# Row statistics between value remainders, and a deferred log of the forget gates, in a hybrid attention layer

## The chip, the cores and the metric

The kernel runs on one core of a Trainium2 chip. The metric is the device time of one execution in microseconds (us); lower is better. The engines are PE (TensorE, matrix products; PEld is its loading of weights), DVE (VectorE), ACT (ScalarE), POOL (GpSimd) and SP (SyncE, which here issues DMAs). Each takes its own instructions in order, and semaphores join them. "The profile" is one execution recorded by the chip's profiler; lines such as L516 are lines of the kernel before.

## What is computed

One layer of a streaming encoder on a sequence of 1024 rows of width 1024, in float32: a modulated layer norm, one input projection, two groups of eight attention heads of width 64 (forgetting attention and stick-breaking attention), a gate on each head, an output projection, and a layer norm over the residual. Cut to what matters:

```python
mod = silu(c) @ w_ada + b_ada                      # shift, scale, gate
u = layer_norm(x) * (1 + scale) + shift
fq, fk, fv, fg, ff, sq, sk, sv, sg = split(u @ w_in)
log_f = log_sigmoid(ff + b_f)                      # 8 forget gates for each row
f_cum = cumsum(log_f, axis=1)
# forgetting attention, causal:   softmax(q k / 8 + f_cum[q] - f_cum[k]) v
# stick-breaking, strictly causal: z = q k / 8
#   w = exp(log_sigmoid(z) + sum of log_sigmoid(-z) over later keys);  w v
y = concat(fox * silu(fg), sb * silu(sg)) @ w_out
x = layer_norm(2 ** 0.25 * x + gate * y, ln_g, ln_b)
```

## The kernel before

**Precision.** Every float32 product is made of three or four passes over split operands: a rounded high part and a remainder. The rounding is a copy on ACT (sometimes POOL), the remainder a subtraction on DVE or POOL. A result in a bank of PSUM is therefore read first by ACT (rounded part) and then by DVE (accumulator minus rounded part). Two readers of one bank take turns.

**Order.** The order on PE is as the program is written, from start to end (`manual_schedule`); that on SP too, up to L856. On ACT, DVE and POOL a planner that simulates the time line at build picks the order among the instructions that it takes to be ready. `after(a, b)` adds an edge without a semaphore: what is issued inside stands, on the engine of `a`, behind `a`. It fixes an order and nothing more.

**The start.** Eight row tiles of 128 rows of x. For each, `norm_stats(t)` takes two `bn_stats` halves of 512 columns and one aggregate on DVE (L197, L198, L189), then the inverse square root on POOL (L191, L192), and `norm_x(t)` normalises in place, on DVE for tiles 6 and 7 (L217), else on ACT (L218). Tiles 0 to 3 make the first half of u, over which five projection accumulators are built (loop at L683, `start_steps`). In that loop's step `kb == 5` stand the statistics of tiles 4 and 5, in step 6 those of tiles 6 and 7, behind the step's last remainder `rest`. Then PE makes the values of row tiles 0 to 3 (`v_first`, L798 to L810). One such block is 24 matmuls (L355 to L357). Its evacuation is four instructions in turn: rounding on ACT (L363), remainder on DVE (L364), for each of two head pairs; they are put into `v_evacs`. Blocks 0 and 2 lie in the two halves of the tile `st_late`, block 1 in one of two "T" banks. Between the blocks stand `norm_x(5..7)`, behind `v_evacs` of block 0, and `late_round(0)` and `late_round(1)`: four transposes of tiles 4 to 7 (L242) each, into T banks, rounded on ACT and DVE. The second of these takes the T bank of value block 1.

**The main loop** runs over 128 units (pair, head, row tile i). For a unit k of the first four pairs (stick-breaking) PE first transposes the weights of unit k-2 (L514, at most four blocks to a T bank, two T banks), with a weights-times-values product (L531) in between, and then makes the scores S of unit k (L462, L463). Two sigmoids on ACT (L484, L486) empty S, a scan on DVE (L491, L495) and a product on POOL (L497) make the weights. The transposes are rounded on ACT (L516), and their remainder is taken on DVE (L517), which frees the T bank. S has one buffer: the next unit's scores wait for both sigmoids. Behind each unit come filler steps: the remaining projections, cut into steps of three matmuls by generators (`gen_m`: two empty steps, then 16; `gen_v`). `FILL` sets the steps of each pair (52, 72, 68, 68, ...), spread over its 16 units about evenly (`W0` = 100), `LEAD` = 2 half units ahead.

**The forget gates.** `gen_forget` runs beside the projections of pairs 2 and 3, one of its steps after each of theirs. Its input `fsb` is complete with the last value block of group 1 (filler step 122). It takes max(-f, f) on DVE (L388), then a sigmoid and its logarithm on ACT (L389, L390; the logarithm isn't in the table of functions that the sigmoid uses, so ACT loads another, and loads the first back at the next sigmoid), waits `FLOG` = 8 steps, adds min(f, 0) (L394) and scans over row tiles (L397), waits `FROW` = 16 steps, builds a triangle of ones on POOL in a slot of the ring that the attention tiles use (L401 to L405), sums over rows on PE (L407, L408), transposes (L414), and stores the sums to DRAM from SP (L416). They are read back when pair 4 begins.

Of the kernel before, what the change touches and what calls it, by code (L numbers as in the profile page):

```python
# [10 lines left out]
AF = mybir.ActivationFunctionType  # L11
# [16 lines left out]
def tile_hybrid_layer(  # L28
# [17 lines left out]
    nc = tc.nc  # L46
# [9 lines left out]
    def att_tile(name, dt=F32):  # L56
        return big("att", 6, name, dt)
# [10 lines left out]
    def t_tile(name):  # L68
        return ps.tile([P, 512], F32, tag="T", bufs=2, name=name)

    def s_tile(name):
        return ps.tile([P, 2, 512], F32, tag="S", bufs=1, name=name)

    RING = 5
    WARM = (4, 1, 1, 1, 1)
    NORM_ON = {6: nc.vector, 7: nc.vector}
    FLOG = 8
    FROW = 16
    GATE = 20
# [3 lines left out]
    def after(*instructions):  # L83
        stack = ExitStack()
        for i in instructions:
            stack.enter_context(tc.issue_after(i.ins))
        return stack
# [54 lines left out]
    c_sb = cp.tile([P, NB], F32, tag="c_sb", name="c_sb")  # L142
    xt, wss_sb, late_x = [], [], []
# [22 lines left out]
    cm = cp.tile([P, NB], F32, tag="cm", name="cm")  # L166
# [15 lines left out]
        nc.tensor.matmul(sc_all[:, kt // 4, kt % 4 * P:][:, :P], sc[:, kt:kt + 1].to_broadcast([P, P]), ident,  # L182
                         start=True, stop=True)

    powed = [None]

    def ln_finish(st, name):
        mv = sb.tile([P, 2], F32, tag="mv", bufs=3, name=f"mv_{name}")
        nc.vector.bn_aggr(mv, st)  # L189
        rs = sb.tile([P, 2], F32, tag="rs", bufs=3, name=f"rs_{name}")  # L190
        nc.gpsimd.tensor_scalar_add(rs[:, 0:1], mv[:, 1:2], EPS)  # L191
        powed[0] = nc.gpsimd.tensor_tensor(rs[:, 0:1], rs[:, 0:1], mhalf, op=ALU.pow)  # L192
        return mv, rs

    def ln_stats(src, name):
        st = sb.tile([P, 3, 6], F32, tag="st", bufs=3, name=f"st_{name}")[:, :2, :]
        nc.vector.bn_stats(st[:, 0, :], src[:, 0:512])  # L197
        nc.vector.bn_stats(st[:, 1, :], src[:, 512:1024])  # L198
        return ln_finish(st, name)


# [3 lines left out]

    norm = {}

    def norm_stats(t):
        mv, rs = norm[t] = ln_stats(xt[t], f"a{t}")
        if t not in NORM_ON:  # L210
            nc.gpsimd.tensor_scalar(rs[:, 1:2], mv[:, 0:1], rs[:, 0:1], -1.0, op0=ALU.mult, op1=ALU.mult)

    def norm_x(t, a=0, b=D):
        mv, rs = norm[t]
        xs = xt[t][:, a:b]
        if t in NORM_ON:
            return NORM_ON[t].tensor_scalar(xs, xs, mv[:, 0:1], rs[:, 0:1], op0=ALU.subtract, op1=ALU.mult)  # L217
        return nc.scalar.activation(xs, xs, AF.Identity, scale=rs[:, 0:1], bias=rs[:, 1:2])  # L218
# [4 lines left out]
    def in_turn(make, *args):  # L223
        with after(*turn_of):
            turn_of[:] = [make(*args)]
        return turn_of[0]
# [116 lines left out]
    v_evacs = []  # L343
# [40 lines left out]
    def gen_forget():  # L384
        ff = fsb.rearrange("p h t -> p (h t)")
        ab = cp.tile([P, 64], F32, tag="fab", name="fab")
        lf = flf[:, 1:]
        nc.vector.scalar_tensor_tensor(ab, ff, -1.0, ff, op0=ALU.mult, op1=ALU.max)  # L388
        nc.scalar.activation(ab, ab, AF.Sigmoid)  # L389
        nc.scalar.activation(ab, ab, AF.Ln)  # L390
        for _ in range(FLOG):
            yield
        with after(*lows):
            nc.vector.scalar_tensor_tensor(lf, ff, 0.0, ab, op0=ALU.min, op1=ALU.add)  # L394

        pre = ff
        nc.vector.tensor_tensor_scan(pre, flf[:, 0:64], later.rearrange("p h t -> p (h t)"), initial=0.0,  # L397
                                     op0=ALU.add, op1=ALU.mult)
        for _ in range(FROW):
            yield  # L400
        scratch = att_tile("fscratch")  # L401
        tri, fr = scratch[:, :P], scratch[:64, P:2 * P]
        nc.gpsimd.memset(tri, 1.0)
        nc.gpsimd.affine_select(out=tri, in_=tri, pattern=[[1, P]], base=0,
                                channel_multiplier=-1, compare_op=ALU.is_ge, fill=0.0)  # L405
        fp = t_tile("fcum")[:, :64]
        nc.tensor.matmul(fp, tri, lf, start=True, stop=False)  # L407
        nc.tensor.matmul(fp, ones.to_broadcast([P, P]), pre, start=False, stop=True)  # L408
        fc = cp.tile([P, 64], F32, tag="fab", name="fc")
        nc.scalar.activation(fc, fp, AF.Copy, scale=-1.0)  # L410
        yield
        yield
        ft = t_tile("frow")[:64, :P]
        nc.tensor.transpose(ft, fc, ident)  # L414
        nc.scalar.copy(fr, ft)
        nc.sync.dma_start(f_dr.rearrange("h (t p) -> (h t) p", p=P), fr)  # L416
        yield
# [17 lines left out]
        r = slice(h * HD, h * HD + HD)  # L435
        nc.scalar.copy(z[r, :], qst[p][h].bitcast(F32)[r, i * P:i * P + P])  # L436

    masks, scaled, lows = [], [], []

    def att_causal(u):  # L440
        p, h, i = u
        if p >= 4:
            if not masks:
                masks.append(pv_tile("causal_ps", 1)[:, :P])
                nc.vector.tensor_copy(masks[0], causal)
            f = fb[2 * (p - 4) + h]
            dg = slice(i * P, i * P + P)
            nc.vector.tensor_tensor(f[:, dg], f[:, dg], masks[0], op=ALU.add)

    def att_scores(u, following):  # L450
        p, h, i = u
        z = zq.pop(u)
        ke = (i + 1) * P
        ns = 1 if ke <= 512 else 2
        w = ke // ns
        qs = slice(i * P, i * P + P)
        if p >= 4:
            f = fb[2 * (p - 4) + h]
        S = s_tile(f"S_{p}_{h}_{i}")
        for s in range(ns):  # L460
            ks = slice(s * w, s * w + w)
            nc.tensor.matmul(S[:, s, :w], qst[p][h][:, qs], kst[p][h][:, ks], start=True, stop=False)  # L462
            nc.tensor.matmul(S[:, s, :w], z, klo[p][:, ks], start=False, stop=True)  # L463
        v3 = lambda a: a[:, :ke].rearrange("p (a b) -> p a b", a=ns)
        if p >= 4:
            a = att_tile(f"a_{p}_{h}_{i}")
            nm = sb.tile([P, 1], F32, tag="nm", bufs=4, name=f"nm_{p}_{h}_{i}")
            l = sb.tile([P, 1], F32, tag="l", bufs=4, name=f"l_{p}_{h}_{i}")
            with after(*lows):
                nc.vector.tensor_tensor_reduce(out=v3(a), in0=S[:, :ns, :w], in1=v3(f),  # L470
                                               op0=ALU.add, op1=ALU.min, scale=-1.0, scalar=BIG,
                                               accum_out=nm)
            if following:
                att_causal(following)
            nc.scalar.activation(a[:, :ke], a[:, :ke], AF.Exp, scale=-1.0, bias=nm, accum_out=l)  # L475
            nc.vector.reciprocal(l, l)  # L476
            scaled[:] = [*scaled[-3:],
                         nc.gpsimd.tensor_scalar(a[:, :ke], a[:, :ke], l, 1.0, op0=ALU.mult, op1=ALU.mult)]  # L478
            st_w[u] = a
        else:  # L480
            kp = att_tile(f"kp_{p}_{h}_{i}")
            be = att_tile(f"be_{p}_{h}_{i}")
            with after(*key_casts):
                nc.scalar.activation(v3(kp), S[:, :ns, :w], AF.Sigmoid, scale=-1.0)  # L484
            key_casts.clear()
            last_act = nc.scalar.activation(v3(be), S[:, :ns, :w], AF.Sigmoid)  # L486


            lo = max(ke - 512, 0)
            rv = kp[:, lo:ke][:, ::-1]  # L490
            last_dve = nc.vector.tensor_tensor_scan(rv, rv, floor[:, :ke - lo], initial=0.0,  # L491
                                                    op0=ALU.mult, op1=ALU.max)
            if lo:
                rv = kp[:, :lo][:, ::-1]
                last_dve = nc.vector.tensor_tensor_scan(rv, rv, floor[:, P:P + 1].to_broadcast([P, lo]),  # L495
                                                        initial=kp[:, lo:lo + 1], op0=ALU.mult, op1=ALU.max)
            nc.gpsimd.tensor_tensor(be[:, :ke - 1], be[:, :ke - 1], kp[:, 1:ke], op=ALU.mult)  # L497
            nc.gpsimd.memset(be[:, ke - 1:ke], 0.0)
            st_w[u] = be
            return last_act, last_dve  # L500
# [182 lines left out]
    for kb in range(NB):  # L683
# [18 lines left out]
        else:  # L702
# [3 lines left out]
            rest = in_turn(u_rest, kb + 1)  # L706
# [33 lines left out]
            norm_stats(5)  # L740
            norm_x(4)
        if kb == 6:
            with after(rest):
                for t in (6, 7):
                    norm_stats(t)
            make_v(0)

    wg = {}
# [45 lines left out]
    def v_first(t, acc):  # L794
        for _ in v_tile(0, t, acc, v0_w):
            pass

    v_first(0, late_acc[:, 0, :])  # L798
    with after(*v_evacs):
        for t in (5, 6, 7):  # L800
            norm_x(t)
# [12 lines left out]
    for kb in range(NB):  # L814
# [9 lines left out]
        if kb < len(evacs):  # L824
            n, h = evacs[kb]
# [5 lines left out]
    first = nc.scalar.copy(held[:, :512], acc1[0])  # L831
# [343 lines left out]
```

## Time and profile before

| | us |
|---|---|
| median of 3 runs | 682.38 (682.34 to 682.41) |
| the profiled execution | 682.39 |
| its span, first to last instruction | 680.6 |
| granted clock of PE, mean | 0.997 |
| all waits of PE in its list, sum of five | 3.0 |

A timeline row reads: start, length, engine, line, operation, tile written <- tiles read, shapes, how many instructions are merged, and in brackets the idle time before it with what ended it. The ends of matmuls are modelled (a 128x512 one is listed with 0.39 and the next starts 0.23 later), so distances between starts say more than lengths. A row of the waits reads: who waited for whom, total us, times, the longest. Where a wait is on several semaphores, the one that came last is named, and it need not be the one that mattered.

### The profile page before, as it was taken

What the parts mean: (1) busy time and instruction counts of PE and PEld (TensorE: products, weight loads), DVE (VectorE), ACT (ScalarE), POOL (GpSimd) and SP (SyncE); (2) the same over time, 40 slices, a digit from 0 to 9 for tenths busy, and PEclk for the clock granted to TensorE, in tenths of its full rate; (3) what the DMA queues carried; (4) which work ended last, traced back from release to release, by engine and by line L of the source; (5) the groups of instructions that cost most, each with busy time, mean ns of one, the idle gap of its engine ahead of it and who ended that gap; (6) DMA issues with size and microseconds to landing.
All of it is one profiled execution on the core that took longest, in us unless ns stands there. A gap on an engine that the chain in (4) does not pass through costs nothing.

```text
span 680.6 us, 11191 instructions
## 1 busy us (share of the span) xinstructions
PE 670.2 (98%) x3713; PEld 571.7 (84%) x3713; DVE 484.8 (71%) x996; ACT 380.1 (56%) x857; POOL 406.1 (60%) x530
## 2 busy tenths in 40 slices
PE   8999999999999999999999999999999999999995
PEld 5788898888997888889988888889988888888885
DVE  6787779868666777777676675766676777885645
ACT  6567368756566666666665564656565766521000
POOL 5550279756357656566369778786795365655412
PEclk9999999999999999999999999999999999999998
DMA  9983432112102122122134454363352297153301
GB/s 332 401 309 117 140 76 77 41 29 59 34 11 66 41 54 56 40 54 55 32 109 144 147 165 156 106 192 118 118 178 59 60 361 299 59 178 105 119 32 62
DMA packets 46472, 81.54 MB, mean 120 GB/s; under 512 B 5264, under 2 KB 20176, under 8 KB 46416
## 3 DMA queue, kind: packets, MB, share of 16 engines
q1 hardware_dynamic: 44832, 76.37, 34.6%
q10 hardware_dynamic: 1584, 4.47, 2.1%
q8 instruction: 29, 0.48, 0.3%
q14 instruction: 27, 0.22, 0.1%
HBM read 60.34 MB, written 16.29 MB: 113 GB/s over the span
## 4 chain that ended last, share of the span: by engine, by line
PE 94%; DVE 2%; ACT 1%; POOL 1%; issue 0%; POOLq 0%; DVEq 0%
PE m L297 10%; PE m L298 10%; PE m L299 10%; PE pv L531 10%; PE T L514 9%; PE S L463 5%; PE S L462 5%; PE o L917 4%; PE o L915 4%; PE o L916 4%; PE v L355 4%; PE v L357 4%; PE v L356 4%; PE st_late L623 1%; PE st_q L623 1%; PE sc_all L176 1%
## 5 line engine op out<-in xcount | busy, mean ns | idle before, releaser
L517 DVE TENSOR_TENSOR pt<-T,pt 128x512 fp32r<-128x512 f32 (+2 forms) x192 | 102.6, 553 | 43.2 <-ACT pt L516 41.7
L516 ACT CAST pt<-T 128x512 fp32r<-128x512 f32 (+2 forms) x192 | 88.7, 478 | 64.3 <-PE T L514 62.5
L297 PE MATMUL m<-uh,whi 128*128 128x512 f32 x304 | 123.4, 406 | 0.0
L299 PE MATMUL m<-uh,wlo 128*128 128x512 f32 x304 | 119.8, 394 | 0.0
L298 PE MATMUL m<-ul,whi 128*128 128x512 f32 x304 | 119.6, 394 | 0.0
L497 POOL TENSOR_TENSOR be<-be,kp 128x127 f32<-128x127 f32 (+3 forms) x64 | 79.0, 1235 | 37.4 <-DVE kp L495 25.8
L491 DVE TENSOR_TENSOR_SCAN kp<-kp,floor 128x512 f32<-128x512 f32 (+2 forms) x64 | 65.0, 1016 | 25.5 <-ACT kp L484 24.4
L531 PE MATMUL pv<-pt,v 128*128 128x512 f32 x320 | 82.8, 388 | 0.0
L478 POOL TENSOR_SCALAR a<-a,l 128x1024 f32<-128x1024 f32 (+3 forms) x64 | 48.4, 757 | 36.5 <-DVE l L476 27.8
L462 PE MATMUL S<-k,q 128*128 128x512 f32 (+5 forms) x192 | 68.8, 360 | 0.3 <-ACT be L486 0.3
L299 PEld LDWEIGHTS m<-uh,wlo 128*128 128x128 f32 x304 | 57.1, 188 | 13.7
L475 ACT ACTIVATE a<-a,nm 128x1024 f32<-128x1024 f32 (+3 forms) x64 | 49.8, 778 | 29.2 <-DVE nm L470 28.8
L297 PEld LDWEIGHTS m<-uh,whi 128*128 128x128 f32 x304 | 57.2, 188 | 10.1 <-PE T L514 0.3
L463 PE MATMUL S<-kl,qz 128*128 128x512 f32 (+5 forms) x192 | 65.3, 341 | 0.0
L298 PEld LDWEIGHTS m<-ul,whi 128*128 128x128 f32 x304 | 57.3, 188 | 9.0
L531 PEld LDWEIGHTS pv<-pt,v 128*128 128x128 f32 x320 | 55.4, 189 | 9.1
L547 POOL TENSOR_TENSOR ty<-ty,sg 64x256 f32<-64x256 f32 x64 | 47.0, 734 | 24.0 <-issue 11.0
L470 DVE CUSTOM_DVE_ANT_0 a<-S,fb 128x1024 f32<-128x1024 f32 (+3 forms) x64 | 48.2, 753 | 16.8 <-PE S L463 13.1
L436 ACT CAST qz<-q 64x128 fp32r<-64x128 f32 x128 | 37.3, 296 | 33.9 <-PE S L463 32.7
L355 PE MATMUL v<-whi_v,uh 128*128 128x256 f32 (+1 forms) x192 | 54.7, 285 | 0.0
L357 PE MATMUL v<-wlo_v,uh 128*128 128x256 f32 (+1 forms) x192 | 54.2, 282 | 0.0
L484 ACT ACTIVATE kp<-S 128x128 f32<-128x128 f32 (+3 forms) x64 | 42.0, 656 | 21.5 <-PE S L463 20.2
(289 smaller groups left out, 1622.6 us busy)
## 6 DMA issues: line engine op xcount, KB each, us to landing
raw<-in_w_qkg_dram SPq DMA_DIRECT2D x38, 256.0 KB, 2.8
wss<-in_w_ss_dram SPq DMA_DIRECT2D x16, 512.0 KB, 8.5
x<-in_x_dram SPq DMA_DIRECT2D x8, 512.0 KB, 6.6
k<-k SPq DMA_DIRECT2D x32, 128.0 KB, 2.3
wg<-in_w_gate_dram SPq DMA_DIRECT2D x8, 512.0 KB, 4.6
raw_o<-in_w_out_dram SPq DMA_DIRECT2D x16, 256.0 KB, 2.9
fb<-f_dr ACTq DMA_DIRECT2D x8, 512.0 KB, 4.4
wo_dr<-whi_o SPq DMA_DIRECT2D x16, 256.0 KB, 2.1
```

The source lines that it names most:

```text
L297: nc.tensor.matmul(acc, hi[:, c], u_hi[kt][:, s], start=(kt == 0), stop=False)
L298: nc.tensor.matmul(acc, hi[:, c], u_lo[kt][:, s], start=False, stop=False)
L299: nc.tensor.matmul(acc, lo[:, c], u_hi[kt][:, s], start=False, stop=(kt == NB - 1))
L355: nc.tensor.matmul(acc[:, :n], u_hi[kt][:, ts_], hi[:, s], start=(kt == 0), stop=False)
L357: nc.tensor.matmul(acc[:, :n], u_hi[kt][:, ts_], lo[:, s], start=False, stop=(kt == NB - 1))
L462: nc.tensor.matmul(S[:, s, :w], qst[p][h][:, qs], kst[p][h][:, ks], start=True, stop=False)
L463: nc.tensor.matmul(S[:, s, :w], z, klo[p][:, ks], start=False, stop=True)
L491: last_dve = nc.vector.tensor_tensor_scan(rv, rv, floor[:, :ke - lo], initial=0.0, op0=ALU.mult, op1=ALU.max)
L497: nc.gpsimd.tensor_tensor(be[:, :ke - 1], be[:, :ke - 1], kp[:, 1:ke], op=ALU.mult)
L516: nc.scalar.copy(hi[:, :n, qo:qo + P], t3)
L517: lows[:] = [nc.vector.tensor_tensor(lo[:, :n, qo:qo + P], t3, hi.bitcast(F32)[:, :n, qo:qo + P], op=ALU.subtract)]
L531: nc.tensor.matmul(acc2[:, :, q0:], vt[p][:, kb, h * P:(h + 1) * P], pt[:, :, q0:], start=(kb == 0), stop=(kb == last))
```

## The change

Two edits. First, the statistics at the start. The two halves of `ln_stats` can each be put behind instructions of their own. Tile 6's statistics stand behind tile 5's aggregate as well; tile 7's leave the loop and come after the first value block: the first half behind that block's first remainder (`v_evacs[1]`) and tile 6's aggregate, the second half behind its second remainder (`v_evacs[3]`).

```diff
-    powed = [None]
+    powed, aggr = [None], [None]
     def ln_finish(st, name):
...
-        nc.vector.bn_aggr(mv, st)
+        aggr[0] = nc.vector.bn_aggr(mv, st)
...
-    def ln_stats(src, name):
+    def ln_stats(src, name, behind):
         st = sb.tile([P, 3, 6], F32, tag="st", bufs=3, name=f"st_{name}")[:, :2, :]
-        nc.vector.bn_stats(st[:, 0, :], src[:, 0:512])
-        nc.vector.bn_stats(st[:, 1, :], src[:, 512:1024])
+        for h, first in enumerate(behind):
+            with after(*first):
+                nc.vector.bn_stats(st[:, h, :], src[:, h * 512:h * 512 + 512])
         return ln_finish(st, name)
...
-    def norm_stats(t):
-        mv, rs = norm[t] = ln_stats(xt[t], f"a{t}")
+    def norm_stats(t, *behind):
+        mv, rs = norm[t] = ln_stats(xt[t], f"a{t}", behind or ((), ()))
...
         if kb == 6:
-            with after(rest):
-                for t in (6, 7):
-                    norm_stats(t)
+            with after(rest, aggr[0]):
+                norm_stats(6)
             make_v(0)
...
     v_first(0, late_acc[:, 0, :])
+    norm_stats(7, (v_evacs[1], aggr[0]), (v_evacs[3],))
     with after(*v_evacs):
```

Second, the forget gates. The sigmoid and the logarithm come seven filler steps later, behind the latest unit's second sigmoid (`gates`, set in `att_scores`), and a small sigmoid of 8 columns, whose result nobody reads, is issued behind the logarithm. All that follows in `gen_forget` moves by the same seven steps.

```diff
+    FGATE = 7
...
         nc.vector.scalar_tensor_tensor(ab, ff, -1.0, ff, op0=ALU.mult, op1=ALU.max)
-        nc.scalar.activation(ab, ab, AF.Sigmoid)
-        nc.scalar.activation(ab, ab, AF.Ln)
+        for _ in range(FGATE):
+            yield
+        with after(*gates):
+            nc.scalar.activation(ab, ab, AF.Sigmoid)
+            logs = nc.scalar.activation(ab, ab, AF.Ln)
+        with after(logs):
+            nc.scalar.activation(cm, c_sb, AF.Sigmoid)
         for _ in range(FLOG):
             yield
...
-    masks, scaled, lows = [], [], []
+    masks, scaled, lows, gates = [], [], [], []
...
             last_act = nc.scalar.activation(v3(be), S[:, :ns, :w], AF.Sigmoid)
+            gates[:] = [last_act]
```

## The prediction

> **What bounds the kernel now.** I read the page's busy times first, then the waits of PE over the whole span.
>
> ```profile
> PE 670.2 (98%) x3713; PEld 571.7 (84%) x3713; DVE 484.8 (71%) x996; ACT 380.1 (56%) x857; POOL 406.1 (60%) x530
> PE sc_all L176 <- POOL ident masks.py:199: 1.6, 1, 1.6
> PE st_late L355 <- DVE v L364: 0.5, 1, 0.5
> PE st_q L623 <- ACT uh L255: 0.3, 1, 0.3
> PE T L514 <- POOL wlo L127: 0.3, 1, 0.3
> PE S L462 <- ACT be L486: 0.3, 1, 0.3
> ```
>
> PE is busy 98% of the span, and all that it waits for is five places. Its instructions run in the order in which they are written, so a wait that goes shortens the span by its length, unless PE then meets another. Two places belong to the change: the value block at 51 us (L355) and the pair L514, L462 near 213 us. A listed wait counts from a modelled end. What PE really loses I take from starts in the timeline of PE. First the value blocks of 24 matmuls each:
>
> ```profile
> 44.79 0.28 PE L355 MATMUL st_late<-v_home,uh 128*128 128x256 f32 x1
> ...
> 47.63 0.28 PE L355 MATMUL v<-v_home,uh 128*128 128x256 f32 x1
> ...
> 50.37 0.28 PE L357 MATMUL v<-v_w,uh 128*128 128x256 f32 x1
> 51.15 0.39 PE L355 MATMUL st_late<-v_home,uh 128*128 128x256 f32 x1 [0.50 <-DVE v L364]
> ...
> 54.09 1.03 PE L242 MATMUL xT<-ident,x 128*128 128x128 f32 x8
> ```
>
> The block of row tile 0 takes 47.63 - 44.79 = 2.84, which is 0.12 a matmul. Tile 2's block should start at 50.37 + 0.12 = 50.49 and end at 53.33. It ends at 54.09, so **0.76 us** are lost here. Then the second place, beside the same step one pair later:
>
> ```profile
> 212.20 0.40 PE L299 MATMUL m<-uh,wlo 128*128 128x512 f32 x1
> 212.89 1.06 PE L514 MATMUL T<-ident,be 128*128 128x128 f32 x8 [0.30 <-POOL wlo L127]
> ...
> 214.56 0.40 PE L297 MATMUL m<-uh,whi 128*128 128x512 f32 x1
> ...
> 247.11 0.40 PE L299 MATMUL m<-uh,wlo 128*128 128x512 f32 x1
> ...
> 248.46 0.40 PE L297 MATMUL m<-uh,whi 128*128 128x512 f32 x1
> ...
> 251.24 0.27 PE L514 MATMUL T<-ident,be 128*128 128x128 f32 x1
> ```
>
> From the last projection matmul over eight transposes and two score matmuls to the next projection it is 214.56 - 212.20 = 2.36 here and 248.46 - 247.11 = 1.35 there: **1.01 us** lost. Both places together are 1.77 of 682.39, 0.26%. That is the ceiling of the change; 0.2% (1.36 us) is about what a measurement of this kernel can tell from no change.
>
> **Part 1, the statistics.** Next the timelines of DVE, ACT and POOL at the first place.
>
> ```profile
> 47.60 0.69 DVE L197 BATCH_NORM_STATS2 st_a<-x 128x6 f32<-128x512 f32 x1
> ...
> 48.81 0.19 DVE L189 BATCH_NORM_AGGREGATE mv_a<-st_a 128x2 f32<-128x12 f32 x1
> ...
> 49.47 0.68 DVE L198 BATCH_NORM_STATS2 st_a<-x 128x6 f32<-128x512 f32 x1
> 50.18 0.29 DVE L364 TENSOR_TENSOR v<-st_late,v 128x128 fp32r<-128x128 f32 x1
> ...
> 50.80 0.29 DVE L364 TENSOR_TENSOR v<-st_late,v 128x128 fp32r<-128x128 f32 x1
> 51.62 1.70 DVE L217 TENSOR_SCALAR x<-x,mv_a,rs_a 128x1024 f32<-128x1024 f32 x2 [0.53 <-POOL rs_a L192]
> ...
> 53.85 0.29 DVE L364 TENSOR_TENSOR v<-v,v 128x128 fp32r<-128x128 f32 x1 [0.33 <-ACT v L363]
> ```
>
> ```profile
> 50.50 0.27 ACT L363 CAST v<-st_late 128x128 fp32r<-128x128 f32 x1 [2.00 <-DVE v L364]
> ```
>
> ```profile
> 51.02 1.45 POOL L192 TENSOR_TENSOR rs_a<-rs_a,mhalf 128x1 f32<-128x1 f32 x2
> ```
>
> Four statistics halves (tiles 6 and 7) stand ahead of the first value remainder at 50.18. The second value rounding on ACT waits 2.00 for that remainder, since both read one bank, and the second remainder at 50.80 lets PE go at 51.15, 0.35 after its start. The change removes no instruction and adds none. Tile 5's aggregate goes ahead of tile 6's halves, and tile 7's halves go one behind each remainder. New order on DVE from 47.60: aggregate 5 (0.1 to 0.2), two halves of tile 6 (48.81 - 47.60 = 1.21), so the first remainder starts at about 49.0. ACT's second rounding (0.27) lies beside aggregate 6 (0.2) and the first half of tile 7 (0.68). The second remainder starts near 50.1, and PE may go at 50.1 + 0.35 = 50.45, before its 50.49. The wait goes.
>
> What is late next: PE reaches the eight transposes (L242) 0.76 earlier, at 53.33. The first four read tiles 4 to 7 normalised; the next four write the bank that the remainders of tile 1's values empty, about 0.4 later (half of the eight), at 53.73. From 50.1 DVE still has a remainder (0.29), a half (0.68), aggregate 7 (0.2), two normalisations (1.70) and two remainders (0.58): 3.45, so 53.55 without a gap. Tile 7's scale passes POOL behind aggregate 7 (about 51.2): half of 1.45 for the power, with the addition ahead of it ready near 52.2, so tile 7's normalisation can't end before 53.05. With PE's 0.35 behind the start of the last remainder (53.26) it goes on at 53.6 without gaps on DVE, and at 54.1 if DVE idles 0.5, as it does at 51.62. I take a new wait of 0.2 there: **gain 0.55**, bounds 0 (DVE's chain ends when it did) and 0.76. No DMA is moved in this part.
>
> **Part 2, the logarithm.** ACT and DVE at the second place, and ACT and DVE one pair later:
>
> ```profile
> 209.72 0.26 ACT L389 ACTIVATE fab<-fab 128x64 f32<-128x64 f32 x1 [2.97 <-DVE fab L388]
> 209.99 1.28 ACT L390 ACT_TABLE_LOAD   x1
> ...
> 211.45 0.95 ACT L516 CAST pt<-T 128x512 fp32r<-128x512 f32 x2
> 212.42 1.28 ACT L484 ACT_TABLE_LOAD   x1
> 213.72 0.28 ACT L484 ACTIVATE kp<-S 128x128 f32<-128x128 f32 x1
> ...
> 214.78 0.59 ACT L289 ACTIVATE sg<-m 128x512 f32<-128x512 f32 x1
> ...
> 245.77 0.30 ACT L436 CAST qz<-q 64x128 fp32r<-64x128 f32 x1
> 247.98 1.08 ACT L516 CAST pt<-T 128x512 fp32r<-128x512 f32 x2 [1.91 <-PE T L514]
> ```
>
> ```profile
> 212.05 1.16 DVE L517 TENSOR_TENSOR pt<-T,pt 128x512 fp32r<-128x512 f32 x2 [2.37 <-ACT pt L516]
> ...
> 248.60 1.29 DVE L517 TENSOR_TENSOR pt<-T,pt 128x512 fp32r<-128x512 f32 x2 [1.33 <-ACT pt L516]
> ```
>
> ACT takes instructions in order. The small sigmoid L389 waits 2.97 on DVE, then comes the load for the logarithm, and only at 211.45 the roundings of transposed weights that stand behind them. Their remainders run from 212.05, the first over at about 212.7, and only then has PE a free transpose bank: 212.89. (The wait list names a POOL split; no transpose reads one, and the bank explains the time as well.) The load back, 1.28 at 212.42, holds the sigmoids that empty S, so L462 waits too.
>
> New: the log of the gates began in filler step 123; seven later is step 130, and by FILL and W0 that is the first step behind unit (2,0,0)'s scores (124 steps through pair 1, some 4 for each unit, LEAD half units ahead), so it stands behind that unit's second sigmoid. The block is sigmoid, load, logarithm, load, small sigmoid: 0.26 + 1.28 + 0.26 + 1.28 + at most 0.26 = 3.3 in a row. The added sigmoid costs between 0 and 0.26; I take 0.2. What covers it is the gap that ACT has one pair later at the same spot: from 245.77 + 0.30 to 247.98, 1.91. The rest, 3.3 - 1.9 = 1.4, pushes the roundings behind it. One pair later their first remainder ends at about 248.60 + 0.65 = 249.25, and PE wants the bank at 251.24: 2.0 of slack against 1.4. So 0.6 is left, and none if the tanh of the gate projection (L289, 0.59) also goes ahead. **Gain 0.95**, bounds 0 (the pair of loads is merely moved) and 1.01. The row-sum step (matmuls L407, transpose L414, store to f_dr on SP) moves seven steps too; its matmuls cost PE the same there, and its store is wanted when pair 4 begins.
>
> The page ScalarE: Activation LUTs of the Trainium skill, section What ACT_TABLE_LOAD costs, speaks against this part: it puts a switch at 1.28 of load and 1.38 of drain, 2.66 in all. By that the block would be an estimated 6.1, and the sum would lose some 2 us to a new wait of PE. In the rows the load starts at 209.99, when L389 ends (209.98), and L484 starts at 213.72, when its load ends (213.70), so I use 1.28.
>
> **Sum.** 682.39 - 0.55 - 0.95 = 680.9 (span 679.1). The profiled execution's 682.39 is 0.01 off the median 682.38, so the sum needs no shift.
>
> **Rivals.**
> 1. The start's gain is caught at the transposes: DVE's remainder at 53.85 stays where it is. For it: DVE has only 0.2 to spare of the new times. Against: it idled 0.53 and 0.33 in this stretch. Part 2 alone: 681.4. Chance 0.17.
> 2. The logarithm isn't hidden, the two loads come apart again (the planner may set the small sigmoid behind the next roundings), and PE waits as before: 682.39 - 0.55 = 681.8. Chance 0.14. With it goes a longer switch: if ACT empties ahead of each load and a load costs its 1.28 twice, the roundings come 2 x 1.28 = 2.6 later still, 2.0 beyond the 0.6 that is left: 682.39 - 0.55 - 1.01 + 2.0 = 682.8. Chance 0.03, as the rows show no gap. That is what the page's drain would do.
> 3. Slower: the triangle for the row sums (L403, L404 on POOL) moves to unit (2,0,5) and gets behind that unit's product.
>
> ```profile
> 226.33 0.29 POOL L404 TENSOR_SCALAR_AFFINE_SELECT fscratch<-fscratch 128x128 f32<-128x128 f32 x1
> ...
> 234.05 1.55 POOL L497 TENSOR_TENSOR be<-be,kp 128x767 f32<-128x767 f32 x1 [1.33 <-DVE kp L495]
> ...
> 236.27 1.31 POOL L127 TENSOR_TENSOR wlo<-raw,whi 128x512 fp32r<-128x512 f32 x1
> ```
>
> ```profile
> 233.40 0.39 PE L299 MATMUL m<-uh,wlo 128*128 128x512 f32 x1
> ```
>
> PE wants it at 233.40 + 0.23 = 233.6 on the old clock. Behind the product it is ready no earlier than 235.60 + 0.29 = 235.9, behind the split 237.58 + 0.29 = 237.9: 2.3 to 4.3 lost on top of the forecast, 683.2 to 685.2. It decides once the triangle ends after 233.6. Against: POOL idles 1.33 ahead of the product, and what is ready goes first. Chance 0.08, 0.06 of it above 683.75.
> 4. The planner's new orders on ACT, DVE and POOL open small waits elsewhere that eat the gain, or the instructions don't land where the edges point: 682.3. Chance 0.10, 0.01 beyond +0.2%.
>
> **How the numbers follow.** The forecast, both parts with at least 1.36 of 1.77 kept, has 0.48. Faster by over 0.2% is that alone, 0.48; slower 0.06 + 0.01 = 0.07; the rest, rivals 1, 2 and most of 4, 0.45. The low end is the ceiling, 682.39 - 1.77 = 680.6, less 0.1. The high end takes in rivals 1 and 2 and half of 4: 682.4. Outside lie the 0.08 of rival 3, the 0.03, half of rival 4 and a little below.
>
> **What would show it.** In PE's waits the rows L355 at 51 and L514 and L462 at 213 are gone; on DVE a half of tile 7 stands between the two remainders; the block start-to-start of tile 2 is 2.84. A wait of L242 at 53.4 would be rival 1. On ACT both loads should stand between two sigmoids with no rounding between; a wait of PE at L514 near 216 would be rival 2, one of L407 rival 3. The forecast is wrong if PE, with these rows gone, waits anywhere else for a microsecond.

## The result, and the profile after

The changed kernel takes 680.91 us (median of 10 runs, 680.42 to 681.46) against 682.43 for the kernel before (10 runs, 682.33 to 683.04): ratio 0.9976, 95% interval 0.9968 to 0.9984. The forecast was 680.9, faster by over 0.2%; the ratio gives 0.24%, its interval 0.16% to 0.32%. All medians here are of fast executions; two slow ones of the kernel before (946.36 and 2126.95 us, beside e5 to e8) are left out. The lines of the changed kernel are numbered a little higher: L242 is now L244, L355 is L357, L462 is L469, L514 is L522, L516 and L517 are L524 and L525.

First the page's span and busy times, and all that PE waits for:

```profile
span 678.7 us, 11184 instructions
PE 669.4 (99%) x3713; PEld 571.8 (84%) x3713; DVE 485.2 (71%) x996; ACT 380.3 (56%) x858; POOL 405.3 (60%) x530
```

```profile
PE sc_all L177 <- POOL ident masks.py:199: 1.6, 1, 1.6
PE st_q L631 <- ACT uh L257: 0.3, 1, 0.3
```

The three waits behind 14 us are gone, and no other has come. The timeline of PE at the two places, start, length, engine, line, operation:

```profile
50.38 0.28 PE L359 MATMUL v<-v_w,uh 128*128 128x256 f32 x1
50.50 0.28 PE L357 MATMUL st_late<-v_home,uh 128*128 128x256 f32 x1
...
53.36 1.03 PE L244 MATMUL xT<-ident,x 128*128 128x128 f32 x8
54.15 0.37 PE L357 MATMUL v<-v_home,uh 128*128 128x256 f32 x1
```

```profile
211.44 0.40 PE L301 MATMUL m<-uh,wlo 128*128 128x512 f32 x1
211.68 1.03 PE L522 MATMUL T<-ident,be 128*128 128x128 f32 x8
...
212.79 0.40 PE L299 MATMUL m<-uh,whi 128*128 128x512 f32 x1
...
215.34 0.40 PE L301 MATMUL m<-uh,wlo 128*128 128x512 f32 x1
215.59 0.30 PE L522 MATMUL T<-ident,be 128*128 128x128 f32 x1
```

Tile 2's value block begins 0.12 behind the last matmul of tile 1's and lasts 53.36 - 50.50 = 2.86, 2.98 together; before it was 0.78 + 2.94 = 3.72. That is 0.74 us. At the second place the stretch is 212.79 - 211.44 = 1.35 against 2.36: 1.01 us. DVE at the first place:

```profile
47.64 0.21 DVE L190 BATCH_NORM_AGGREGATE mv_a<-st_a 128x2 f32<-128x12 f32 x1
47.77 1.23 DVE L200 BATCH_NORM_STATS2 st_a<-x 128x6 f32<-128x512 f32 x2
49.03 0.29 DVE L366 TENSOR_TENSOR v<-st_late,v 128x128 fp32r<-128x128 f32 x1
49.24 0.20 DVE L190 BATCH_NORM_AGGREGATE mv_a<-st_a 128x2 f32<-128x12 f32 x1
49.35 0.64 DVE L200 BATCH_NORM_STATS2 st_a<-x 128x6 f32<-128x512 f32 x1
49.91 0.27 DVE L366 TENSOR_TENSOR v<-st_late,v 128x128 fp32r<-128x128 f32 x1
...
51.53 0.24 DVE L366 TENSOR_TENSOR v<-v,v 128x128 fp32r<-128x128 f32 x1
52.10 0.29 DVE L366 TENSOR_TENSOR v<-v,v 128x128 fp32r<-128x128 f32 x1 [0.33 <-ACT v L365]
52.67 0.81 DVE L219 TENSOR_SCALAR x<-x,mv_a,rs_a 128x1024 f32<-128x1024 f32 x1 [0.28 <-POOL rs_a L193]
```

The order is the one written: aggregate 5, tile 6, remainder, aggregate 6, one half of tile 7, remainder. The second remainder starts at 49.91 in place of 50.80. Further down, what the prediction didn't foresee: tile 1's two remainders (51.53, 52.10) go ahead of tile 7's normalisation, so the bank for the second four transposes is free early. ACT at the second place:

```profile
210.12 0.26 ACT L394 ACTIVATE fab<-fab 128x64 f32<-128x64 f32 x1
210.28 0.28 ACT L443 CAST qz<-q 64x128 fp32r<-64x128 f32 x1
210.58 1.28 ACT L395 ACT_TABLE_LOAD   x1
211.87 0.26 ACT L395 ACTIVATE fab<-fab 128x64 f32<-128x64 f32 x1
212.13 1.28 ACT L397 ACT_TABLE_LOAD   x1
213.43 0.21 ACT L397 ACTIVATE cm<-c_sb 128x8 f32<-128x8 f32 x1
213.54 0.58 ACT L291 ACTIVATE sg<-m 128x512 f32<-128x512 f32 x1
214.02 1.07 ACT L524 CAST pt<-T 128x512 fp32r<-128x512 f32 x2
```

Both loads stand between sigmoids. Of roundings only a short one of a query tile (L443) has gone in between, ahead of the first load, and none of transposed weights. The tanh of the gate projection (L291) goes ahead of the roundings, the case in which the prediction left no slack. On POOL the triangle comes ahead of its unit's product, as it must:

```profile
228.99 0.29 POOL L411 TENSOR_SCALAR_AFFINE_SELECT fscratch<-fscratch 128x128 f32<-128x128 f32 x1
...
231.74 1.55 POOL L505 TENSOR_TENSOR be<-be,kp 128x767 f32<-128x767 f32 x1 [1.26 <-DVE kp L503]
```

### The profile page after: what moved, and what is told of

The parts are those of the page before. It is cut to its first block, busy times and chain, and to the rows that moved or that the text cites. A ratio compares the mean times of both kernels' runs of the same rounds, so it can differ in the third digit from the quotient of the medians.

```text
span 678.7 us, 11184 instructions
## 1 busy us (share of the span) xinstructions
PE 669.4 (99%) x3713; PEld 571.8 (84%) x3713; DVE 485.2 (71%) x996; ACT 380.3 (56%) x858; POOL 405.3 (60%) x530
## 4 chain that ended last, share of the span: by engine, by line
PE 98%; POOL 1%; ACT 0%; issue 0%; DVE 0%; POOLq 0%
PE m L299 10%; PE m L300 10%; PE m L301 10%; PE pv L539 10%; PE T L522 9%; PE S L470 5%; PE S L469 5%; PE o L925 4%; PE o L924 4%; PE o L923 4%; PE v L357 4%; PE v L359 4%; PE v L358 4%; PE st_q L631 1%; PE st_k L631 1%; PE st_late L631 1%
## 5 line engine op out<-in xcount | busy, mean ns | idle before, releaser
L525 DVE TENSOR_TENSOR pt<-T,pt 128x512 fp32r<-128x512 f32 (+2 forms) x192 | 102.6, 553 | 41.1 <-ACT pt L524 39.4
L524 ACT CAST pt<-T 128x512 fp32r<-128x512 f32 (+2 forms) x192 | 88.8, 479 | 65.2 <-PE T L522 63.3
L469 PE MATMUL S<-k,q 128*128 128x512 f32 (+5 forms) x192 | 68.8, 360 | 0.0
L443 ACT CAST qz<-q 64x128 fp32r<-64x128 f32 x128 | 37.3, 296 | 33.6 <-PE S L470 32.4
L357 PE MATMUL v<-whi_v,uh 128*128 128x256 f32 (+1 forms) x192 | 54.7, 285 | 0.0
```

Source lines behind the costliest of these rows:

```text
L357: nc.tensor.matmul(acc[:, :n], u_hi[kt][:, ts_], hi[:, s], start=(kt == 0), stop=False)
L524: nc.scalar.copy(hi[:, :n, qo:qo + P], t3)
L525: lows[:] = [nc.vector.tensor_tensor(lo[:, :n, qo:qo + P], t3, hi.bitcast(F32)[:, :n, qo:qo + P], op=ALU.subtract)]
```

## The experiments

The times spread over about a microsecond from one execution to the next, so next to each median stands what PE lost at the places in question in that run's own trace. A is the distance from the last matmul of tile 1's value block to the first of the eight transposes, less 2.97, its shortest value; X is those eight transposes, 0.79 when nothing holds them; B the stretch from the last projection over eight transposes and two scores to the next; T the next transpose behind the last projection, 0.23 to 0.25 when free. V is the start of the first value matmul. Each median is of 10 or 11 executions.

| run | median us | ratio, 95% interval | A lost | X | B | T | V | span |
|---|---|---|---|---|---|---|---|---|
| before (first trace) | 682.43 | | 0.75 | 0.79 | 2.36 | 0.23 | 44.79 | 680.6 |
| the change (first trace) | 680.91 | 0.9976, 0.9968 to 0.9984 | 0.01 | 0.79 | 1.35 | 0.25 | 44.81 | 678.7 |
| e1 the change | 680.97 | 0.9977, 0.9968 to 0.9986 | 0.00 | 0.79 | 1.34 | 0.24 | 44.74 | 679.5 |
| e2 statistics only | 681.95 | 0.9991, 0.9983 to 1.0000 | 0.00 | 0.79 | 2.34 | 0.23 | 44.68 | 679.8 |
| e3 log only | 681.69 | 0.9988, 0.9979 to 0.9996 | 0.75 | 0.79 | 1.35 | 0.24 | 45.33 | 680.1 |
| e4 no small sigmoid | 680.69 | 0.9976, 0.9967 to 0.9984 | 0.00 | 0.79 | 1.35 | 0.24 | 44.82 | 678.7 |
| e5 log not deferred | 682.92 | 1.0006, 0.9997 to 1.0016 | 0.00 | 0.79 | 3.35 | 0.23 | 44.82 | 681.0 |
| e6 both halves before | 681.43 | 0.9983, 0.9974 to 0.9993 | 0.42 | 0.80 | 1.35 | 0.25 | 44.94 | 679.4 |
| e7 one half more on DVE | 681.49 | 0.9984, 0.9974 to 0.9994 | 0.00 | 1.50 | 1.35 | 0.24 | 45.23 | 679.9 |
| e8 seven small sigmoids | 681.77 | 0.9988, 0.9979 to 0.9997 | 0.00 | 0.79 | 1.35 | 1.17 | 44.98 | 679.8 |
| e9 change, early row | 680.98 | 0.9974, 0.9966 to 0.9983 | 0.00 | 0.80 | 1.35 | 0.25 | 45.16 | 679.1 |
| e10 before, early row | 682.66 | 0.9999, 0.9990 to 1.0008 | 0.77 | 0.79 | 2.35 | 0.23 | 45.20 | 680.9 |
| e11 e4 and early row | 681.24 | 0.9978, 0.9969 to 0.9987 | 0.00 | 0.79 | 1.35 | 0.24 | 45.47 | 679.4 |

The kernel before ran beside each: 682.53 with e1 to e4, 682.56 with e5 to e8, 682.67 with e9 to e11.

**e1: the change again.** No edit.

> The changed kernel itself, beside its parts. My theory: the two waits of PE are independent, and each is worth its length from start to start, 0.75 (values) and 1.02 (log), 1.77 together: 680.6 to 681.0, PE's waits after 14 us empty. The first trace shows a span 1.9 shorter than before while the medians differ by 1.52, so single executions may again spread over 680.4 to 681.5.

680.97. A and B as in the first trace, but PE's list of waits isn't empty:

```profile
PE S L469 <- DVE nm L477: 0.6, 1, 0.6
```

It lies at 553 us. DVE's timeline there names a transfer:

```profile
550.72 0.29 DVE L455 TENSOR_TENSOR fb<-fb,causal_ps 128x128 f32<-128x128 f32 x1 [0.99 <-DMA fb<-f_dr]
```

A row of the forget sums, loaded to all partitions, lets DVE start at 550.72 where the first trace has 549.99; there DVE waited 0.19 for it and PE not at all. PE's scores start at 553.31 against 552.58, which is 0.80 late, since this run is 0.07 earlier up to there (V, 44.74 against 44.81). This is what e9 and e10 ask about.

**e2 and e3: one part at a time.** e2 puts the log back, e3 the statistics.

```diff
 # e2, against the change
-        for _ in range(FGATE):
-            yield
-        with after(*gates):
-            nc.scalar.activation(ab, ab, AF.Sigmoid)
-            logs = nc.scalar.activation(ab, ab, AF.Ln)
-        with after(logs):
-            nc.scalar.activation(cm, c_sb, AF.Sigmoid)
+        nc.scalar.activation(ab, ab, AF.Sigmoid)
+        nc.scalar.activation(ab, ab, AF.Ln)
 # e3, against the change
-            with after(rest, aggr[0]):
-                norm_stats(6)
+            with after(rest):
+                for t in (6, 7):
+                    norm_stats(t)
...
-    norm_stats(7, (v_evacs[1], aggr[0]), (v_evacs[3],))
```

> Part 1 alone, the log of the gates as before. Independent waits: 0.75 less than before, 681.65 (0.999); the eight transposes L244 start at 53.36; L514's and L462's counterparts near 212.5 wait as before. Rival (only the later place counts, or what the start gains is caught at the pair near 213): 682.3.

> Part 2 alone, the statistics as before. Independent waits: 1.02 less than before, 681.4 (0.9985); the value block of tile 2 starts at 51.15 again. Rival (the two parts help each other): less than 0.7 off, and e2's and e3's gains don't add up to e1's.

The table shows the parts cleanly apart: e2 has A without loss and B as before, e3 the reverse. By medians e2 is 0.58 and e3 0.84 below the kernel before, 1.42 together, against 1.56 for e1. Both rivals fall: neither wait hides behind the other. PE's list in e2 has one small wait besides, 0.2 at 547 us for a key's remainder. The medians are each less than the 0.75 and 1.01 of the traces; what single executions lose elsewhere is taken up at e9 to e11.

**e4: no small sigmoid.**

```diff
-        with after(logs):
-            nc.scalar.activation(cm, c_sb, AF.Sigmoid)
```

> The change without the small sigmoid behind the log. The order on ACT then shows three table loads instead of two: one for the log, one for the tanh of the gate projection, one for the next unit's sigmoids, behind the two roundings. My theory: the place hides the block, and a third load of 1.28 ahead of the sigmoids of unit (2,0,1) (which ended 1.8 before PE wants S) is hidden as well: 680.9, as the whole change. Rival (the small sigmoid is what hides the load): PE waits at L469 near 217.5, 0.5 to 1.3 more, 681.4 to 682.2.

680.69, not to be told apart from e1. ACT in its trace:

```profile
212.09 1.28 ACT L291 ACT_TABLE_LOAD   x1
...
213.88 1.07 ACT L522 CAST pt<-T 128x512 fp32r<-128x512 f32 x2
214.97 1.28 ACT L489 ACT_TABLE_LOAD   x1
216.26 0.39 ACT L489 ACTIVATE kp<-S 128x256 f32<-128x256 f32 x1
```

Three loads, and PE in step: S is wanted at 217.39, and the second sigmoid ends ahead of it. The place hides the loads; the small sigmoid saves one of them and no time.

**e5: the log not deferred.**

```diff
-    FGATE = 7
+    FGATE = 0
```

> The change with FGATE = 0: sigmoid, log and the added small sigmoid are issued together where the log stood before (behind unit (1,1,6)), ahead of the roundings of unit (1,1,6)'s transposes. My theory: the place is the gain. The block then holds the roundings by 1.28 + 0.1 more than before; PE's L522 near 212 starts about 2.0 late, the second wait (S) goes since the table is back: 681.0 + 2.0 = 683.0, slower than part 1 alone (681.95) by 1. Rival (the small sigmoid brings the gain, by taking the load back off the path of the sigmoids that empty S): 681.4 or less.

682.92, 0.4 above the kernel before, at the edge of what this measures; B shows it plainly, 1.0 more than before and 2.0 more than the change.

```profile
208.93 0.26 ACT L394 ACTIVATE fab<-fab 128x64 f32<-128x64 f32 x1 [2.97 <-DVE fab L390]
209.20 1.28 ACT L395 ACT_TABLE_LOAD   x1
...
212.17 0.95 ACT L524 CAST pt<-T 128x512 fp32r<-128x512 f32 x2
```

```profile
212.77 1.16 DVE L525 TENSOR_TENSOR pt<-T,pt 128x512 fp32r<-128x512 f32 x2 [3.88 <-ACT pt L524]
```

```profile
211.40 0.40 PE L301 MATMUL m<-uh,wlo 128*128 128x512 f32 x1
213.61 1.07 PE L522 MATMUL T<-ident,be 128*128 128x128 f32 x8 [1.81 <-DVE pt L525]
```

ACT stands 2.97 for DVE, then both loads hold the roundings, and PE misses a transpose bank for 2 us. The list now names DVE's remainder L525 as the releaser, where the profile before had named a POOL split: in both traces PE goes on 0.84 behind the start of that remainder (213.61 - 212.77 here, 212.89 - 212.05 before), so the bank was the cause. With e2 and e4 all four cases are there: in the old place B is 2.34 without the small sigmoid and 3.35 with it, in the new place 1.35 either way. The place makes the gain, and in the old place the small sigmoid costs 1.0, as it puts the second load ahead of the roundings too.

**e6: both halves of tile 7 ahead of the second remainder.**

```diff
-            with after(rest, aggr[0]):
-                norm_stats(6)
+            for t in (6, 7):
+                with after(rest, aggr[0]):
+                    norm_stats(t)
...
-    norm_stats(7, (v_evacs[1], aggr[0]), (v_evacs[3],))
```

> The change with both halves of tile 7 between the two value remainders (the aggregates still in turn): one half moves ahead of the second remainder. My theory: the remainder starts 0.55 to 0.6 later (50.5 in place of 49.91) and lets PE go 0.35 behind, at 50.85, so a wait of 0.35 from start to start at the first matmul of the value block L357: 681.3. Rival (the aggregate of tile 5 ahead of tile 6's halves is what counts, not the turns): 50.50 as in the change, 680.95.

681.43. The planner set the first remainder ahead of tile 7 by itself, and the second behind both halves:

```profile
49.49 1.23 DVE L200 BATCH_NORM_STATS2 st_a<-x 128x6 f32<-128x512 f32 x2
50.64 0.28 DVE L366 TENSOR_TENSOR v<-st_late,v 128x128 fp32r<-128x128 f32 x1
```

```profile
50.97 0.39 PE L357 MATMUL st_late<-v_home,uh 128*128 128x256 f32 x1 [0.17 <-DVE v L366]
```

PE goes 0.33 behind the remainder and loses 0.42 of the 0.75. So of part 1's gain about 0.33 comes from the aggregates' order and the first remainder's place, and 0.42 from the turn.

**e7: one half more on DVE.** The second half of tile 7 is taken twice.

```diff
             with after(*first):
-                nc.vector.bn_stats(st[:, h, :], src[:, h * 512:h * 512 + 512])
+                for _ in range(2 if name == "a7" and h == 1 else 1):
+                    nc.vector.bn_stats(st[:, h, :], src[:, h * 512:h * 512 + 512])
```

> The change with one statistics half (0.6) more on DVE ahead of tile 7's aggregate, a repeat of its second half. My theory: tile 7's normalisation, which ends at 53.48 and is wanted by the fourth transpose at 53.69, ends 0.6 to 0.7 later, so PE waits 0.3 to 0.5 within the eight transposes L244: 681.35. Rival (DVE's idle gaps of 0.33 and 0.28 ahead of it take it in, no slack is used up): 680.95, transposes at 53.36 without a wait.

681.49; the transposes take 1.50 in place of 0.79.

```profile
53.89 0.81 DVE L220 TENSOR_SCALAR x<-x,mv_a,rs_a 128x1024 f32<-128x1024 f32 x1 [0.54 <-POOL rs_a L193]
```

```profile
54.76 0.76 PE L245 MATMUL xT<-ident,x 128*128 128x128 f32 x5 [0.49 <-DVE x L220]
```

This run's start lies 0.42 later (its first value matmul at 45.23, the change's at 44.81), so tile 7's normalisation starts 53.89 - 52.67 - 0.42 = 0.80 late (0.61 for the half itself, the rest because a value remainder then goes ahead of the aggregate), and PE loses 0.71. The place named as next late in the prediction is next, with 0.1 of slack: less than the 0.2 that the expectation read.

**e8: seven small sigmoids.**

```diff
-        with after(logs):
-            nc.scalar.activation(cm, c_sb, AF.Sigmoid)
+        last = logs
+        for _ in range(7):
+            with after(last):
+                last = nc.scalar.activation(cm, c_sb, AF.Sigmoid)
```

> The change with seven small sigmoids in place of one, 6 x 0.11 = 0.66 more on ACT behind the log. My theory: this place has no slack left (the first remainder of unit (1,1,7)'s transposes ends at 215.4, PE takes that bank at 215.59), so PE's L522 there starts 0.4 to 0.7 late: 681.5. Rival (half a us or more of slack, as the prediction reckoned without the tanh): 680.95 and L522 in step.

681.77; the transpose at T starts 0.92 late, more than expected.

```profile
213.52 0.69 ACT L399 ACTIVATE cm<-c_sb 128x8 f32<-128x8 f32 x3
214.12 0.58 ACT L291 ACTIVATE sg<-m 128x512 f32<-128x512 f32 x1
214.59 0.68 ACT L399 ACTIVATE cm<-c_sb 128x8 f32<-128x8 f32 x3
215.18 0.57 ACT L526 CAST pt<-T 128x512 fp32r<-128x512 f32 x1
```

```profile
215.45 0.40 PE L301 MATMUL m<-uh,wlo 128*128 128x512 f32 x1
216.62 0.30 PE L524 MATMUL T<-ident,be 128*128 128x128 f32 x1 [0.77 <-DVE pt L527]
```

Six of the seven stand ahead of the first rounding, three on each side of the tanh; that is five more than in the change. Each took about 0.2, not the 0.11 expected, so the pad was larger than meant: the first rounding starts at 215.18 where the change has 214.02, 1.05 later with this run's offset of 0.11 taken off. 1.05 on ACT cost PE 0.92, so this place has a tenth of slack too.

**e9, e10, e11: the row loaded two units earlier**, in the change, in the kernel before, and in e4.

```diff
-            if 4 <= p < NPAIR - 1 and i == 0:
+            if 4 <= p < NPAIR - 1 and i == (2 if (p, h) == (NPAIR - 2, 1) else 0):
```

> The change, and the last load of a forget-gate row (fb, 512 KB, issued behind unit (6,1,0), wanted some 6 us later) issued two units earlier. In the first trace of the change DVE waited 0.19 for this row and PE not; in e1's, 0.99, and PE 0.73 from start to start at the scores near 553. My theory: this load's landing time is much of why single executions of the change spread from 680.4 to 681.5 and why the medians differ by less (1.5) than the traces (1.9). Then the median falls from 680.95 to 680.5 to 680.7, the spread shrinks, and DVE waits for no row near 550. Rival (the spread comes from the start, where PE's wait for the first block differed by 0.5 among traces, or from elsewhere): the median stays at 680.9 within 0.1 and the spread as it was.

> The kernel before with the same earlier load and nothing else. My theory: the same wait is in some executions of the kernel before, fewer of them, as its PE comes later against nothing at this place: its median 682.5 falls by 0.1 to 0.3. Rival (the wait belongs to the change alone): no difference; other rival (the load moves traffic that something else needs): slower.

> The change without the small sigmoid (e4: PE 0.09 earlier at the transpose near 215.6) and with the row loaded early: 680.4 to 680.6, 0.997 of before, if e9 is as expected; else 680.8.

My theory of the spread falls. In the traces of e9 and e11 DVE waits for no row near 550 any more, but e9's median is 680.98 with runs from 680.43 to 681.52, and e10 equals the kernel before. A late row costs 0.8 in an execution that has it, and it isn't what spreads the rest. The traces point to the start instead: V lies anywhere from 44.68 to 45.47, with the same instructions ahead of it on PE. e11's two waits ahead of it, the first of them otherwise in e7's trace alone (0.3):

```profile
PE xT_early L244 <- ACT x L220: 0.7, 1, 0.7
PE st_q L629 <- ACT uh L257: 0.5, 1, 0.5
```

The first is for a row tile that ACT normalises. DVE's timeline shows what comes late ahead of that, the third row tile of x; first the change's first trace, then e11's:

```profile
6.95 1.23 DVE L200 BATCH_NORM_STATS2 st_a<-x 128x6 f32<-128x512 f32 x2
```

```profile
7.89 1.29 DVE L200 BATCH_NORM_STATS2 st_a<-x 128x6 f32<-128x512 f32 x2 [0.77 <-DMA x<-in_x_dram]
```

In e3, e7, e9, e10 and e11 DVE waits 0.17 to 0.77 for the load of this tile, in e6 0.17 for that of the second, and in the other seven traces for neither. V is 44.94 to 45.47 in those six and 44.68 to 44.98 in the seven. A load of x that lands late is thus the likely cause; no run moved it, so it isn't shown by an experiment.

The table also settles what the medians left open. Take from each trace's span its V, its losses in A, X, B and T, e1's 0.80 at the late row, and the 0.2 that e2 and e5 list at 547: 633.9 to 634.1 is left in all thirteen. So, to within that, what is won at the two places reaches the end of the span in full, and nearly all other differences between these spans lie in the first 45 us. No version beats the change by more than this spread.

## Why the prediction was right

**What bounds the kernel.** Right. PE's order is fixed, the two places cost what the distances between starts said (0.76 and 1.01 read, 0.74 and 1.01 gained), and the listed waits (0.5, 0.3, 0.3) would have given too little.

**Part 1.** The order on DVE came out as worked, PE's restart at 50.50 against 50.49. Its gain was mis-sized: 0.55 forecast, 0.74 measured. The term that was wrong is the new wait of 0.2 at the transposes. I had kept tile 1's remainders behind both normalisations; the planner set them ahead of tile 7's, and DVE met both wants of PE. e7 shows that the place is nevertheless the next one.

**Part 2.** The block went where it was worked out to go, behind unit (2,0,0)'s second sigmoid, the tanh ahead of the roundings. 0.95 forecast, 1.01 measured. e5 with e2 and e4 shows that it is the place that hides it, and e8 that a tenth of slack is left, against 0.6 or none in the prediction. The page ScalarE: Activation LUTs of the Trainium skill, section What ACT_TABLE_LOAD costs, would add 1.38 of drain to a switch; here the load starts at 210.58, when the rounding ahead of it ends (210.28 + 0.28 = 210.56), and ends at 210.58 + 1.28 = 211.86; the log starts at 211.87, and the load back at 212.13, when the log ends (211.87 + 0.26). The trace doesn't agree with the drain, and with 0.1 of slack PE would have shown it.

**The sum.** The traces gave 1.75 at the two places (span 1.9 shorter), the sum said 1.5, and the medians fell by 1.52. That the forecast met the median to 0.01 is luck. The sum took off a wait of 0.2 that didn't come, and about as much was lost where it had no term. Over all executions e1's spans are on average 1.65 shorter than those of the kernel before (679.06 against 680.71), 0.1 less than 1.75; late loads, as in the traces of e1 and e11, can account for that. Another 0.1 is lost outside the span: the time beyond it averages 1.82 in the kernel before and 1.92 in e1. It is 1.89 to 1.94 in every version with the deferred log and 1.82 or 1.83 in e2, e5 and e10, which don't have it; no run gives the cause.

**Rivals.** 1 fell with the change's own trace (X 0.79) and e2, 2 with the change's own trace, 3 with the triangle ahead of the product. For 4 there is little: the change's first trace has no new wait, and the 0.6 at 553 in e1 comes and goes from one execution to the next.

## What to carry to other kernels

Where one engine's order is fixed and it is nearly always busy, measure a wait from start to start against the same step elsewhere, not by the listed idle time: here 1.75 won against 1.1 listed. What is to be hidden on another engine has to be put behind the work that the busy engine waits for next and into that engine's own gap; the instructions alone don't hide it (e5). A tenth of slack at the next place is found by padding it, and single executions that spread over more than a gain are compared place by place in their traces.

## What the runs showed of the hardware

A tanh behind the log, without a sigmoid between, loads a table that doesn't serve the next sigmoid: three loads in e4 (one for the log, then those at 212.09 and 214.97) against two. In the kernel before, tanh and sigmoid follow each other without a load. The page ScalarE: Activation LUTs of the Trainium skill, section Table sets: the hidden batching unit, lists tanh both with exp and with sigmoid, which would fit; no run shows which set was loaded.

Small sigmoids that all write the same 8 columns took more in a row than one does alone: in e8 three of them have the next instruction 0.60 behind their start (213.52 to 214.12), and the other three 0.59 (214.59 to 215.18), about 0.2 each, where the change's single one has the tanh 0.11 behind its start. Whether the common output makes the difference wasn't tried.
